# Deeper load buffers in the second expert layer, per-head softmax and early gathers in the routing of a diffusion block

## Chip, cores and metric

One core of a Trainium2 chip runs the whole program. The metric is the device time of one execution in microseconds: the median of three runs is 1841.48 us (1838.68 to 1842.52).

## What is computed

One layer of a diffusion backbone on 512 tokens of width 1024, all in float32. A mixing half (state space heads, long convolutions, output projection) comes first; nothing in it is touched. The second half is a product-key expert layer (PEER): each of 8 heads scores a token against two sets of 128 keys, takes the 16 best of each, the 16 best of the sums, and mixes 16 of 16384 one-neuron experts by a softmax:

```python
q = (hb @ wq).reshape(T, 8, 2, 128)
s1 = einsum('chd,hnd->chn', q[:, :, 0], k1);  s2 = einsum('chd,hnd->chn', q[:, :, 1], k2)
v1, i1 = top_k(s1, 16);  v2, i2 = top_k(s2, 16)
sc, ci = top_k(v1[..., :, None] + v2[..., None, :], 16)     # flattened
e = i1[ci // 16] * 128 + i2[ci % 16];  g = softmax(sc)
act = gelu(einsum('chkd,cd->chk', u_tab[e], hb))
out = einsum('chk,chkd->cd', g * act, v_tab[e])
```

## The kernel before, in words

The expert layer treats two groups of tokens in two ways.

**Tokens 0 to 127 are gathered.** There are 128 slots (8 heads by 16). `gathered(s)` lets GpSimd start an indirect DMA of one row of `uv` (u and v side by side, 8 KB) for each of 128 tokens, 1 MiB in all, into one of three buffers `uvr` (L1429). VectorE forms the dot product with `hrow` (L1430), ScalarE the GELU and the gate (L1433, L1435), VectorE adds the weighted v row to `accg` (L1438). All 128 slots must be done before the end; `gathers(share, after)` hands them out in fractions as the program goes.

**Tokens 128 to 511 are done densely**, over all 128 tiles of 128 experts. `first(i)` loads u tile i (512 KiB), splits it into a high part (ScalarE, L301) and a low part (VectorE, L302) and runs 24 matmuls into `pa` (L306 to L308), then a GELU. `second(i)` loads v tile i into `vr` (L1592), the gates `gc` of four tiles at a time (L1595) and, for a tile whose first layer ran earlier, the stored activations `gal` (L1602); it splits v into `vh` (ScalarE, L1598) and `vl` (VectorE, L1599), forms gate times activation (L1604), splits that into `wwh` and `wwl` (L1607, L1608) and runs 18 matmuls into six accumulators `pacc`.

Four stages follow each other:

1. Routing, eight heads (loop over `hd`): two projections `wq` of 24 matmuls, scores `psc` (L1482), `top16` and `pairs` on VectorE. After each head `run_ahead(RH)` issues `first` for tiles whose activations are stored in DRAM (`GA`), 6.3 a head. After the last head `run_ahead(RS)` adds 4 and one softmax covers all heads; only then is `gidx` (L1453) known and a gather possible.
2. Gates, 96 steps of four tokens: one-hot rows on VectorE and ScalarE (L1549 to L1556), eight matmuls `pgg` (L1558), an eviction to `gst` (L1560), `gathers(G_SHARE)` with 0.23 a step and `run_ahead(RG)` with 0.34 tiles a step. A `first` may come on TensorE no sooner than the `pgg` of three steps before.
3. The second layer over tiles 0 to 87, whose first layer ran ahead (`NRUN` = 88).
4. The second layer over tiles 88 to 127, each with its own `first`, begun two tiles earlier.

In stages 3 and 4 gathers are handed out at `left` a tile, times `R_RUN` in stage 3. `vr` and `gal` have two buffers each. All loads of `second` are issued by SyncE in program order, so a load that waits for its buffer holds back the loads behind it. The framework orders each engine's instructions by a planner with a timeline of its own, mostly in program order; a ready instruction may pass one that waits.

```python
left = (P - due[1] - N_SLACK) / (R_RUN * NRUN + (P - NRUN))
for i in range(P):
    while made < min(P, i + (AHEAD if i >= P - 1 - AHEAD else 2)):
        ready[made] = last_ga = first(made, V)
        made += 1
    last = second(i, ready.pop(i, None))
    gathers(left * (R_RUN if i < NRUN else 1.0) if i < P - 1 else P, last)
```

Of the kernel before, what the change touches and what calls it, by code (L numbers as in the profile page):

```python
# [9 lines left out]
F32 = mybir.dt.float32  # L10
F32R = mybir.dt.float32r
# [3 lines left out]
AF = mybir.ActivationFunctionType  # L15
ALU = mybir.AluOpType
AX = mybir.AxisListType

P = 128
D = 1024  # L20
# [51 lines left out]
          ("bglu", 4), ("gs5", 4), ("ghy", 4), ("negt", 4), ("a_re", 32), ("a_im", 32), ("lstep", 32))  # L72
NG = 128
SG = 32
NRUN = 88
NUV = 3
G_SHARE = 0.23
R_RUN = 0.4
ACT_OH = (2,1)
RG = 0.34  # L80
RH = 6.3
RS = 4
EQ_POOL = 3
G_LAG = 3
# [1 line left out]
ND = L - NG  # L86
# [5 lines left out]
QUIET = 1  # L92
WGT_ACT = 1
RGATE = 0
PERHEAD = 0
GH = 2.0
NOO = 3
S5M = 1
HYAT = 4
GCN = 4  # L100
FQ = 1
MERGE = 1
RECTS = ((0, 1, 16), (1, 1, 8), (2, 2, 5), (4, 4, 3), (8, 8, 1))
NCAND = 54 if MERGE else 50
NVR = 2
NVH = 3
VLV = 2
AHEAD = 2
# [119 lines left out]
def build(tc, I, out, dbg=None, stop=None):  # L228
# [64 lines left out]
    def sm(name, shape, dtype=F32, bufs=1, tag=None):  # L293
        return cur[0].tile(shape, dtype, tag=tag or name, name=name, bufs=bufs)

    def wblock(src, name, lo_eng=None):
# [4 lines left out]
        nc.scalar.activation(hi, raw, AF.Copy)  # L301
        (lo_eng or (nc.vector if FQ else nc.gpsimd)).tensor_tensor(lo, raw, hi.bitcast(F32), ALU.subtract)  # L302
        return hi.rearrange("p (k m) -> p k m", m=P), lo.rearrange("p (k m) -> p k m", m=P)
# [29 lines left out]
    V = nc.vector  # L333
    A = nc.scalar
    GP = nc.gpsimd
    FG = V if FQ else GP
    PE = nc.tensor
# [341 lines left out]
    for part in SEQ.split():  # L679
# [36 lines left out]
        elif part[0] == "S":  # L716
            t0, t1 = ((0, 4), None, (4, 6))[n_]
# [21 lines left out]
        elif part[0] == "P":  # L739
# [5 lines left out]
            if NWARM:  # L745
# [5 lines left out]
                for i in range(NWARM):  # L751
                    mm = PE.matmul(pwarm, warm[:, 0:P], warm, start=True, stop=True)
# [507 lines left out]
    for co in range(4):  # L1260
        wg = sg_(f"wg{co}", [P, 4, P], tag="wg", bufs=2)
        nc.sync.dma_start(wg, I["w_glu"][co].rearrange("p (k m) -> p k m", m=P))
        pg = ps5(f"pg{co}")
# [8 lines left out]
        t = g2_(f"cat5{co}", [P, 512])  # L1272
# [24 lines left out]
    for k in range(8):  # L1297
        t = b2(f"h2t{k}", [P, 512])
# [39 lines left out]
    iotak = sm("iotak", [P, P])  # L1338
# [17 lines left out]

    GA = dram.tile([NRUN, P, ND], F32, name="GA")

# [15 lines left out]
    def run_ahead(share):  # L1374
        ran[0] += share
        while ran[1] < min(NRUN, ran[0]):
            i = ran[1]
# [86 lines left out]
    for hd in range(8):  # L1464
# [20 lines left out]
        last = pairs(hd, val, idx)  # L1485
        if PERHEAD:
            softmax(hd)
            gathers(GH if hd else 0, last)
        run_ahead(RH)

# [4 lines left out]
    def columns(lt, eid, gt):  # L1495

        ei = sm(f"ei{lt}", [P, 2, P], I32, tag="ei", bufs=2)
        V.tensor_copy(ei[:, 0], eid)
        V.tensor_scalar(ei[:, 1], ei[:, 0], 127, None, ALU.bitwise_and)
        V.tensor_scalar(ei[:, 0], ei[:, 0], 7, None, ALU.logical_shift_right)  # L1500
        ef = sm(f"ef{lt}", [P, 2, P], tag="ef", bufs=2)
        V.tensor_copy(ef, ei)
        ptr = ps.tile([P, 512], F32, tag="psc", name=f"ptr{lt}", bufs=2 if RGATE else 3)[:, 0:3 * P].rearrange("p (e n) -> p e n", e=3)
        PE.transpose(ptr[:, 0], ef[:, 0], ident)
        PE.transpose(ptr[:, 1], ef[:, 1], ident)
        PE.transpose(ptr[:, 2], gt, ident)
        if RGATE:
            t = sm(f"cols{lt}", [P, 2, P], tag="cols", bufs=3)
            A.activation(t, ptr[:, 0:2], AF.Copy)
            g = sm(f"colg{lt}", [P, 2, P], F32R, tag="colg", bufs=3)  # L1510
            A.activation(g[:, 0], ptr[:, 2], AF.Copy)
            V.tensor_tensor(g[:, 1], ptr[:, 2], g[:, 0].bitcast(F32), ALU.subtract)
            return t, g.bitcast(F32)
        t = sm(f"cols{lt}", [P, 5, P], tag="cols", bufs=3)
        A.activation(t[:, 0:3], ptr, AF.Copy)
        A.activation(t[:, 3:5], ptr[:, 0:3:2], AF.Copy, scale=-1.0)
        return t

    def gates_r(b_, cols, c0):
        cols, g = cols  # L1520
        st = sm(f"gst{b_}", [P, P, SG], tag="gst", bufs=2)
        for q in range(SG // 4):
            pg = ps.tile([P, 4, 2, P], F32, tag="pgg", name=f"pgg{b_}_{q}", bufs=2)
            t0 = c0 + 4 * q
            oo = sm(f"oo{b_}_{q}", [P, 4, 2, P], F32R, tag="oo", bufs=NOO)
            os_ = sm(f"os{b_}_{q}", [P, 4, 2, P], F32R, tag="os", bufs=NOO)
            V.tensor_tensor(oo, iotak.unsqueeze(1).unsqueeze(1).broadcast_to((P, 4, 2, P)),
                            cols[:, :, t0:t0 + 4].rearrange("p e t -> p t e").unsqueeze(3).broadcast_to((P, 4, 2, P)), ALU.is_equal)
            for e in range(4):
                for h in range(2):  # L1530
                    A.activation(os_[:, e, h], oo[:, e, 0].bitcast(F32), AF.Copy, scale=g[:, h, t0 + e:t0 + e + 1])
            for e in range(4):
                mm = PE.matmul(pg[:, e].rearrange("p h i -> p (h i)"), oo[:, e, 1], os_[:, e].rearrange("p h i -> p (h i)"), start=True, stop=True)
            groups.append(mm)
            so = st[:, :, 4 * q:4 * q + 4]
            A.activation(so, pg[:, :, 0].rearrange("p t i -> p i t"), AF.Copy)
            last = V.tensor_tensor(so, pg[:, :, 1].rearrange("p t i -> p i t"), so, ALU.add)
            gathers(G_SHARE, last)
            run_ahead(RG)
        nc.scalar.dma_start(GD[b_], st)  # L1540

    def gates(b_, cols, c0):
        st = sm(f"gst{b_}", [P, P, SG], tag="gst", bufs=2)
        for q in range(SG // 4):
# [16 lines left out]
            gathers(G_SHARE, last)  # L1561
            run_ahead(RG)
        nc.scalar.dma_start(GD[b_], st)

    run_ahead(RS)
    if not PERHEAD:
        softmax(None)
# [5 lines left out]
    cols = [columns(lt, eids[:, lt], gts[:, lt]) for lt in range(1, 4)]  # L1573
    for lt in range(1, 4):
        for b_ in range(P // SG):
            (gates_r if RGATE else gates)((lt - 1) * (P // SG) + b_, cols[lt - 1], b_ * SG)
    run_ahead(NRUN)
    fr.close()
# [3 lines left out]
    mp = ms.enter_context(tc.tile_pool(name="mp", bufs=2))  # L1582
# [6 lines left out]
    def second(i, ga):  # L1589
        nonlocal gc  # L1590
        vr = mp.tile([P, D], F32, tag="vr", name=f"vr{i}", bufs=NVR)
        nc.sync.dma_start(vr, I["uv"][i * P:(i + 1) * P, D:2 * D])  # L1592
        if i % GCN == 0:
            gc = mp.tile([P, ND // SG, GCN, SG], F32, tag="gc", name=f"gc{i}")
            nc.sync.dma_start(gc, GD[:, :, i:i + GCN, :].rearrange("b p i t -> p b i t"))  # L1595
        vh = mp.tile([P, D], F32R, tag="vh", name=f"vh{i}", bufs=NVH)
        vl = mp.tile([P, D], F32R, tag="vl", name=f"vl{i}", bufs=NVH)
        A.activation(vh, vr, AF.Copy)  # L1598
        (V if QUIET or i >= P - VLV else GP).tensor_tensor(vl, vr, vh.bitcast(F32), ALU.subtract)  # L1599
        if ga is None:  # L1600
            ga = mp.tile([P, ND], F32, tag="gal", name=f"gal{i}")
            nc.sync.dma_start(ga, GA[i])  # L1602
        gw = mp.tile([P, ND], F32, tag="gw", name=f"gw{i}")
        V.tensor_tensor(gw.rearrange("p (b t) -> p b t", t=SG), ga.rearrange("p (b t) -> p b t", t=SG), gc[:, :, i % GCN], ALU.mult)  # L1604
        wh = mp.tile([P, ND], F32R, tag="wwh", name=f"wwh{i}", bufs=NVH)
        wl = mp.tile([P, ND], F32R, tag="wwl", name=f"wwl{i}", bufs=NVH)
        A.activation(wh, gw, AF.Copy)  # L1607
        last = V.tensor_tensor(wl, gw, wh.bitcast(F32), ALU.subtract)  # L1608
        held.append((i, wh, wl, vh, vl))
        if i < P - HOLD or i == P - 1:  # L1610
            for t in range(NT):
                ts_ = slice(t * P, (t + 1) * P)
                for e in range(2):
                    es_ = slice(e * 512, (e + 1) * 512)
                    for (n, ah_, al_, bh_, bl_) in held:
                        mm3(pacc[t][e], (ah_[:, ts_], al_[:, ts_]), (bh_[:, es_], bl_[:, es_]), n == 0, n == P - 1)
            held.clear()
        return last
# [4 lines left out]
    for e in range(2):  # L1623
# [5 lines left out]
        A.activation(gx2[:, e * 512:(e + 1) * 512], pgx, AF.Copy)  # L1629
    left = (P - due[1] - N_SLACK) / (R_RUN * NRUN + (P - NRUN))  # L1630
    ready = {}
    made = NRUN
    for i in range(P):
# [3 lines left out]
        last = second(i, ready.pop(i, None))  # L1637
        gathers(left * (R_RUN if i < NRUN else 1.0) if i < P - 1 else P, last)

# [4 lines left out]
    def residual(t):  # L1644
        xr = mp.tile([P, D], F32, tag="xf", name=f"xf{t}", bufs=4)
        nc.sync.dma_start(xr, X1R[t * P:(t + 1) * P])
        y = mp.tile([P, D], F32, tag="yf", name=f"yf{t}")
        ssq = mp.tile([P, 4], F32, tag="ssq", name=f"ssq{t}", bufs=4)
        for e in range(2):
            V.tensor_tensor(y[:, hs[e]], accg[:, hs[e]] if t == 0 else pacc[t - 1][e], gx2[:, hs[e]], ALU.mult)  # L1650
            (GP if t in T_ADD else V).tensor_tensor(xr[:, hs[e]], y[:, hs[e]], xr[:, hs[e]], ALU.add)
            A.activation(junk[:, hs[e]], xr[:, hs[e]], AF.Square, accum_out=ssq[:, e:e + 1])
        ends.append((xr, ssq))
# [44 lines left out]
```

## Time and profile before

| | |
|---|---|
| median of three runs | 1841.48 us |
| profiled execution | 1842.49 us |
| its span, first to last instruction | 1840.7 us |
| TensorE, matmul / weight load busy | 92% / 77% of the span |
| VectorE, ScalarE, GpSimd busy | 81%, 45%, 9% |
| DMA | 436.13 MB, mean 237 GB/s |
| mean granted TensorE clock | 0.968 of full speed |

The sum of the prediction is made against the profiled execution, which is 1.8 us longer than its span and 1.0 us longer than the median. "Busy" is the time in which at least one instruction of an engine ran; overlapping matmuls count once, so their pitch (start to start) is read from a timeline. A wait names the instruction that was late and what released it.

### The profile page before, as it was taken

How to read it: one execution, taken by the hardware profiler on the slowest of the kernel's cores; microseconds unless marked ns; L12 is line 12 of the kernel's file. 1: busy time of each engine (PE TensorE's matmuls, PEld its weight loads, DVE VectorE, ACT ScalarE, POOL GpSimd, SP SyncE). 2: the span in 40 equal slices, each digit the busy share in tenths (PEclk: the TensorE clock that was granted, in tenths of full speed). 3: DMA queues.
4: the chain of work that ended last, by engine and by line, in shares of the span. 5: the costliest groups of instructions: out<-in, count | busy, mean ns of one | idle time of the engine just before them, and what ended most of it. 6: DMA issues, size and time to landing. Idle time of an engine off the chain costs nothing.

```text
span 1840.7 us, 24953 instructions
## 1 busy us (share of the span) xinstructions
PE 1692.0 (92%) x8729; PEld 1420.7 (77%) x8731; DVE 1492.1 (81%) x3039; ACT 821.4 (45%) x1616; POOL 157.6 (9%) x158
## 2 busy tenths in 40 slices
PE   5799998879999999999999898989898898999997
PEld 2477654447799999989999886767676777999996
DVE  8866999967689988899999766777787777888886
ACT  3444453134533332348988633343333343444444
POOL 0000000000000000001101101111111112121211
PEclk9899998989899999999999998999999999999998
DMA  9436452322444444466898998999989888999981
GB/s 373 146 99 205 160 173 53 75 71 84 126 151 148 146 148 135 145 233 251 325 335 320 341 350 296 311 331 315 331 311 336 302 279 328 360 329 341 342 312 58
DMA packets 170228, 436.13 MB, mean 237 GB/s; under 512 B 17139, under 2 KB 102004, under 8 KB 150902
## 3 DMA queue, kind: packets, MB, share of 16 engines
q1 hardware_dynamic: 128854, 251.28, 40.6%
q0 software_dynamic: 18432, 134.23, 20.2%
q10 hardware_dynamic: 22816, 49.03, 7.3%
q8 instruction: 69, 1.13, 0.2%
q14 instruction: 57, 0.47, 0.1%
HBM read 381.52 MB, written 52.92 MB: 236 GB/s over the span
## 4 chain that ended last, share of the span: by engine, by line
PE 47%; DVE 13%; DMA 13%; ACT 2%; issue 2%; DVEq 0%; ACTq 0%; SPq 0%
DMA vr<-in_uv_dram 11%; PE pa L308 7%; PE pa L306 6%; PE pa L307 6%; PE pacc L307 5%; PE pacc L306 5%; PE pgg L1558 5%; PE pacc L308 5%; DVE vl L1599 2%; PE pq L308 2%; PE pq L306 2%; PE pq L307 2%; ACT vh L1598 2%; DVE idx L1351 1%; DVE rs L1349 1%
## 5 line engine op out<-in xcount | busy, mean ns | idle before, releaser
L307 PE MATMUL pacc<-vl,wwh 128*128 128x512 f32 x768 | 305.8, 399 | 4.7 <-DVE vl L1599 4.7
L308 PE MATMUL pacc<-vh,wwl 128*128 128x512 f32 x768 | 298.0, 397 | 0.0
L306 PE MATMUL pacc<-vh,wwh 128*128 128x512 f32 x768 | 237.1, 402 | 42.8 <-ACT vh L1598 42.7
L1429 POOL DMA_INDIRECT uvr<-in_uv_dram,gidx x128 | 145.2, 1134 | 1148.1 <-DVE accg L1438 810.5
L1599 DVE TENSOR_TENSOR vl<-vr,vh 128x1024 fp32r<-128x1024 f32 x128 | 156.1, 1222 | 94.8 <-ACT vh L1598 94.6
L306 PEld LDWEIGHTS pacc<-vh,wwh 128*128 128x128 f32 x768 | 144.7, 192 | 83.2 <-ACT vh L1598 55.2
L1598 ACT ACTIVATE vh<-vr 128x1024 fp32r<-128x1024 f32 x128 | 135.0, 1057 | 162.3 <-DMA vr<-in_uv_dram 126.5
L307 PEld LDWEIGHTS pacc<-vl,wwh 128*128 128x128 f32 x768 | 148.0, 193 | 38.1 <-DVE vl L1599 7.4
L308 PEld LDWEIGHTS pacc<-vh,wwl 128*128 128x128 f32 x768 | 147.6, 192 | 31.1
L1438 DVE SCALAR_TENSOR_TENSOR accg<-uvr,wgt,accg 128x1024 f32<-128x1024 f32 x128 | 163.7, 1279 | 4.0 <-ACT wgt L1435 1.2
L1430 DVE SCALAR_TENSOR_TENSOR junk<-uvr,hrow 128x1024 f32<-128x1024 f32 x128 | 155.9, 1218 | 2.2 <-DMA uvr<-in_uv_dram,gidx 2.2
L1607 ACT ACTIVATE wwh<-gw 128x384 fp32r<-128x384 f32 x128 | 66.5, 520 | 131.7 <-PE pacc L307 92.3
L1558 PE MATMUL pgg<-o,o 128*128 128x128 f32 x768 | 95.3, 278 | 4.3 <-ACT o L1554 4.3
L1558 PEld LDWEIGHTS pgg<-o,o 128*128 128x128 f32 x768 | 94.3, 195 | 4.5 <-ACT o L1554 4.5
L1608 DVE TENSOR_TENSOR wwl<-gw,wwh 128x384 fp32r<-128x384 f32 x128 | 70.8, 553 | 32.8 <-ACT wwh L1607 32.7
L1549 DVE TENSOR_TENSOR o<-iotak,cols 128x512 f32<-128x512 f32 x96 | 65.9, 686 | 10.3 <-PE pgg L1558 10.3
L1556 DVE TENSOR_SCALAR o<-iotak,cols 128x128 f32<-128x128 f32 x240 | 70.2, 343 | 0.0
L1433 ACT ACTIVATE wgt<-dots 128x1 f32<-128x1 f32 x128 | 25.4, 199 | 87.4 <-DVE junk L1430 87.1
L1554 ACT ACTIVATE o<-o,cols 128x128 f32<-128x128 f32 x144 | 63.6, 493 | 0.2
L1368 ACT ACTIVATE ga<-pa 128x384 f32<-128x384 f32 x128 | 60.4, 472 | 2.7 <-PE pa L308 2.7
L1560 ACT ACTIVATE gst<-pgg 128x512 f32<-128x512 f32 x96 | 56.7, 591 | 2.5 <-PE pgg L1558 2.2
L1604 DVE TENSOR_TENSOR gw<-gal,gc 128x384 f32<-128x384 f32 x88 | 48.4, 553 | 9.1 <-DMA gal<-GA 8.6
(1812 smaller groups left out, 4141.4 us busy)
## 6 DMA issues: line engine op xcount, KB each, us to landing
vr<-in_uv_dram SPq DMA_DIRECT2D x128, 512.0 KB
GD<-gst ACTq DMA_DIRECT2D x12, 2048.0 KB
gc<-GD SPq DMA_DIRECT2D x32, 768.0 KB
GA<-ga ACTq DMA_DIRECT2D x88, 192.0 KB
gal<-GA SPq DMA_DIRECT2D x88, 192.0 KB
wb<-in_w_ada_dram SPq DMA_DIRECT2D x32, 512.0 KB
wa<-in_w_ada_dram SPq DMA_DIRECT2D x8, 1024.0 KB
KD<-kk SPq DMA_DIRECT2D x16, 256.0 KB
```

The costliest lines, as they stand in the source:

```text
L306: nc.tensor.matmul(o, a[0], b[0], start=start, stop=False)
L307: nc.tensor.matmul(o, a[0], b[1], start=False, stop=False)
L308: nc.tensor.matmul(o, a[1], b[0], start=False, stop=stop_)
L1429: GP.indirect_dma_start(out=uvr, out_offset=None, in_=I["uv"], in_offset=bass.IndirectOffsetOnAxis(ap=gidx[:, s:s + 1], axis=0))
L1430: ins = V.scalar_tensor_tensor(junk, uvr[:, 0:D], 1.0, hrow, ALU.mult, ALU.mult, accum_out=dots[:, s:s + 1])
L1438: V.scalar_tensor_tensor(accg, uvr[:, D:2 * D], wgt[:, s:s + 1], accg, ALU.mult, ALU.add)
L1556: last = V.tensor_scalar(o1[:, e], iotak, cols[:, 0, t:t + 1], cols[:, 2, t:t + 1], ALU.is_equal, ALU.mult)
L1558: mm = PE.matmul(pg[:, e, :], o2[:, e], o1[:, e], start=True, stop=True)
L1598: A.activation(vh, vr, AF.Copy)
L1599: (V if QUIET or i >= P - VLV else GP).tensor_tensor(vl, vr, vh.bitcast(F32), ALU.subtract)
L1607: A.activation(wh, gw, AF.Copy)
L1608: last = V.tensor_tensor(wl, gw, wh.bitcast(F32), ALU.subtract)
```

## The change

The constants are edited, `PERHEAD` is switched on, `gal` gets four buffers by `NGAL` and `vr` four by `NVR`; the residual's `yf` (two buffers of its own before) now takes turns in those of `vr`. `gates_r` and the branch of `columns` under `RGATE` are rewritten too, but `RGATE` stays 0, so neither is called.

```diff
-NRUN = 88
+NRUN = 92
-R_RUN = 0.4
+R_RUN = 0.35
-RG = 0.34
-RH = 6.3
+RG = 0.4
+RH = 7
-PERHEAD = 0
-GH = 2.0
+PERHEAD = 1
+GH = 3
+NGAL = 4
-NVR = 2
+NVR = 4
...
         if RGATE:
...
     def gates_r(b_, cols, c0):
...
         if ga is None:
-            ga = mp.tile([P, ND], F32, tag="gal", name=f"gal{i}")
+            ga = mp.tile([P, ND], F32, tag="gal", name=f"gal{i}", bufs=NGAL)
             nc.sync.dma_start(ga, GA[i])
...
-        y = mp.tile([P, D], F32, tag="yf", name=f"yf{t}")
+        y = mp.tile([P, D], F32, tag="vr", name=f"yf{t}", bufs=NVR)
```

With `PERHEAD` the loop over heads runs, after `pairs(hd)`, the softmax of that head alone (six VectorE operations and an Exp) and `gathers(3 if hd else 0, last)`; the softmax over all heads at the end falls away. `GH` was without effect before.

## Rows read from the trace of the kernel before

**Rows 1.** The page's slices: GB/s moved in each of 40 equal slices.

```profile
GB/s 373 146 99 205 160 173 53 75 71 84 126 151 148 146 148 135 145 233 251 325 335 320 341 350 296 311 331 315 331 311 336 302 279 328 360 329 341 342 312 58
```

**Rows 2.** Busy time by stage: routing, gates, turn, run tiles, tiles with their own first.

```profile
core 0: us, PE busy (x) PEld busy (x) DVE busy (x) ACT busy (x) POOL busy (x), PEclk, DMA share, GB/s
488.00:806.00 318.00, 314.81 (x1738) 297.49 (x1736) 279.21 (x991) 103.68 (x141) 0.38 (x2) 1.00 0.44 145
806.00:1047.00 241.00, 236.48 (x1618) 235.84 (x1617) 227.19 (x466) 204.44 (x507) 30.22 (x26) 0.99 0.85 313
1047.00:1062.00 15.00, 6.15 (x32) 5.61 (x31) 2.28 (x6) 2.03 (x3) 0.29 (x1) 0.81 0.92 322
1062.00:1500.00 438.00, 396.63 (x1682) 320.47 (x1682) 318.62 (x428) 162.20 (x287) 52.27 (x51) 0.96 0.93 321
1500.00:1820.00 320.00, 313.80 (x1556) 282.28 (x1555) 256.83 (x321) 141.00 (x268) 62.43 (x51) 0.99 0.85 305
```

**Rows 3.** Waits between 1062 and 1535 us: total us, times, longest.

```profile
ACT vh L1598 <- DMA vr<-in_uv_dram: 124.3, 61, 9.6
PE pacc L306 <- ACT vh L1598: 42.7, 27, 5.5
```

**Rows 4.** Waits of SyncE's DMA queue between 1062 and 1535 us.

```profile
SPq L1592 <- DVE vl L1599: 151.4, 79, 5.8
```

**Rows 5.** Chain of waits near 1340 us: start, us, what.

```profile
1339.63 1.24 DVE vl L1599
1340.88 6.26 DMA vr<-in_uv_dram
1347.16 1.07 ACT vh L1598
```

**Rows 6.** Busy time by stage, instructions on the tile pacc alone.

```profile
1062.00:1500.00 438.00, 372.22 (x1539) 294.35 (x1540) 0.00 (x0) 0.96 0.93 321
1500.00:1820.00 320.00, 175.60 (x729) 137.54 (x728) 0.00 (x0) 0.99 0.85 305
```

**Rows 7.** Timeline of TensorE: the first matmuls of tiles 94 and 95, and one of pacc before.

```profile
1541.00 0.40 PE L306 MATMUL pacc<-vh,wwh 128*128 128x512 f32 x1
...
1542.37 0.33 PE L306 MATMUL pa<-h2h,u94h 128*128 128x384 f32 x1
...
1546.55 0.33 PE L306 MATMUL pa<-h2h,u95h 128*128 128x384 f32 x1
```

**Rows 8.** Busy time in two heads of six run-ahead tiles each, columns as rows 2.

```profile
563.00:639.60 76.60, 76.01 (x418) 71.50 (x417) 70.44 (x250) 23.44 (x32) 0.00 (x0) 1.00 0.44 145
```

**Rows 9.** Waits of VectorE in the routing, 488 to 806 us.

```profile
DVE val L1346 <- PE psc L1482: 23.4, 8, 3.0
```

**Rows 10.** Groups of the page: the two VectorE passes of a gather.

```profile
L1438 DVE SCALAR_TENSOR_TENSOR accg<-uvr,wgt,accg 128x1024 f32<-128x1024 f32 x128 | 163.7, 1279 | 4.0 <-ACT wgt L1435 1.2
L1430 DVE SCALAR_TENSOR_TENSOR junk<-uvr,hrow 128x1024 f32<-128x1024 f32 x128 | 155.9, 1218 | 2.2 <-DMA uvr<-in_uv_dram,gidx 2.2
```

**Rows 11.** Timeline of the softmax over all heads, and a VectorE cast of 64 elements.

```profile
798.84 1.28 ACT L1447 ACT_TABLE_LOAD   x1
798.87 0.67 DVE L1446 TENSOR_TENSOR GX<-SC 128x512 f32<-128x512 f32 x1
...
799.46 0.19 DVE L1412 CAST posf<-pos 128x64 f32<-128x64 uint32 x1
...
800.13 0.63 ACT L1447 ACTIVATE GX<-GX 128x512 f32<-128x512 f32 x1
```

**Rows 12.** Gates: two pieces of the chain of waits (start, us).

```profile
921.60 2.68 PE pgg L1558 x24
928.47 2.68 PE pgg L1558 x24
```

**Rows 13.** Gates: VectorE's one-hot rows, a group of the page and a timeline piece.

```profile
L1549 DVE TENSOR_TENSOR o<-iotak,cols 128x512 f32<-128x512 f32 x96 | 65.9, 686 | 10.3 <-PE pgg L1558 10.3
...
901.56 0.85 DVE L1556 TENSOR_SCALAR o<-iotak,cols 128x128 f32<-128x128 f32 x3
```

More of the change, by code (lines that the diff above doesn't have):

```diff
@@ L1507, in columns @@
         if RGATE:
[L1508 to L1513, printed above, removed]
+            t = sm(f"cols{lt}", [P, P], tag="cols", bufs=3)
+            A.activation(t, ptr[:, 1], AF.Copy)
+            gh_ = sm(f"colg{lt}", [P, P], F32R, tag="colg", bufs=3)
+            A.activation(gh_, ptr[:, 2], AF.Copy)
+            V.tensor_tensor(ptr[:, 2], ptr[:, 2], gh_.bitcast(F32), ALU.subtract)
+            return t, gh_.bitcast(F32), ptr
         t = sm(f"cols{lt}", [P, 5, P], tag="cols", bufs=3)
@@ L1519, in gates_r, with per_token @@
     def gates_r(b_, cols, c0):
-        cols, g = cols
+        i2, gh_, ptr = cols
         st = sm(f"gst{b_}", [P, P, SG], tag="gst", bufs=2)
+        def per_token(x, t0):
+            return x[:, t0:t0 + 4].unsqueeze(2).broadcast_to((P, 4, P))
         for q in range(SG // 4):
@@ L1524, in gates_r @@
             t0 = c0 + 4 * q
-            oo = sm(f"oo{b_}_{q}", [P, 4, 2, P], F32R, tag="oo", bufs=NOO)
+            o2 = sm(f"o2_{b_}_{q}", [P, 4, P], F32R, tag="o2", bufs=NOO)
+            o1 = sm(f"o1_{b_}_{q}", [P, 4, P], tag="o1", bufs=NOO)
             os_ = sm(f"os{b_}_{q}", [P, 4, 2, P], F32R, tag="os", bufs=NOO)
-            V.tensor_tensor(oo, iotak.unsqueeze(1).unsqueeze(1).broadcast_to((P, 4, 2, P)),
-                            cols[:, :, t0:t0 + 4].rearrange("p e t -> p t e").unsqueeze(3).broadcast_to((P, 4, 2, P)), ALU.is_equal)
+            keys_ = iotak.unsqueeze(1).broadcast_to((P, 4, P))
+            GP.tensor_tensor(o2, keys_, per_token(i2, t0), ALU.is_equal)
+            V.tensor_tensor(o1, keys_, per_token(ptr[:, 0], t0), ALU.is_equal)
+            V.tensor_tensor(os_[:, :, 1], o1, per_token(ptr[:, 2], t0), ALU.mult)
             for e in range(4):
-                for h in range(2):
-                    A.activation(os_[:, e, h], oo[:, e, 0].bitcast(F32), AF.Copy, scale=g[:, h, t0 + e:t0 + e + 1])
+                A.activation(os_[:, e, 0], o1[:, e], AF.Copy, scale=gh_[:, t0 + e:t0 + e + 1])
             for e in range(4):
-                mm = PE.matmul(pg[:, e].rearrange("p h i -> p (h i)"), oo[:, e, 1], os_[:, e].rearrange("p h i -> p (h i)"), start=True, stop=True)
+                mm = PE.matmul(pg[:, e].rearrange("p h i -> p (h i)"), o2[:, e], os_[:, e].rearrange("p h i -> p (h i)"), start=True, stop=True)
             groups.append(mm)
```

## The prediction, made before the changed kernel was run

> **What bounds the kernel now.** I read the slices first for where the DMA engines are loaded: in the second half they move 280 to 360 GB/s, in the routing 135 to 150 [rows 1]. Then the busy times by stage [rows 2]. In routing and gates TensorE is busy 99% and 98% of the time: it sets the pace, with VectorE close behind, 88% in the routing and 94% in the gates. From 1062 to 1500 us, over the tiles that ran ahead, no engine is full: DMA 0.93, TensorE 91% by matmul busy but 73% by weight loads. From 1500 us on, where each tile brings its own `first`, TensorE is at 98%.
>
> The third view was the list of waits of that middle stage. ScalarE's `vh` waited 124.3 us for `vr` to land, and TensorE 42.7 us for `vh` [rows 3]; SyncE in turn stood 151.4 us before issuing `vr`, for the `vl` that frees a buffer [rows 4]. The chain shows the loop: `vl` 1.24, load 6.26, `vh` 1.07 us, in all 8.6 us for a buffer, and two buffers give 4.3 us a tile at best [rows 5]. ScalarE waited up to 9.6 us for one load [rows 3], so the average is worse: 1539 matmuls of `pacc` by 1500 us are 85.5 tiles [rows 6], and after an 11 us start they took 427 us: 4.99 us a tile. The last term is TensorE's own price. From 1541.00 to 1542.37 us six matmuls of `pacc` start before the first of tile 94 [rows 7]: a pitch of 0.228 us, and 18 make 4.11 us. A `first` takes 1546.55 - 1542.37 = 4.18 us [rows 7]; of all the matmuls in this stage 143 are not of `pacc` [rows 2, 6], some 5 of them `first` tiles that the planner moved up, two in the start and about 3.5 after it.
>
> **Edit 1, gathers and softmax in the routing.** Heads 1 to 7 each issue three gathers: 21. One costs VectorE 1.22 + 1.28 = 2.50 us [rows 10], three 7.5. A head's softmax is six VectorE operations on 64 elements or fewer; the nearest row has 0.19 us for 64 [rows 11], so about 1.1 us. `RH` 7 makes 56 tiles instead of 51 (0.3 x 8 rounded up): 5 x 4.18 = 21 us of TensorE, and 1.1 us of VectorE for each further low part. A head with six tiles lasts 38.3 us, VectorE busy 35.2 of them [rows 8]. With seven tiles TensorE needs 42.5 us, and VectorE 35.2 + 1.1 + 7.5 + 1.1 = 44.9: **VectorE becomes the bound of the routing.** It can use the 3 us in which it now waits for each head's scores, 23.4 us in all [rows 9], since the gathers stand just there. So 42.5 for head 0 and 7 x 45 = 357.5 us against 318: **+40 us**. Bounds: +23 if VectorE's extra work all found room beside TensorE's; +66 if none of it did (21 x 2.50 + 5 x 1.1 + 8 x 1.1). I stand nearer the middle, since [rows 8] leave VectorE no more than 3 us a head.
>
> The rest of this edit has cover. The 21 MiB of gathers find DMA 0.44 loaded [rows 2]. GpSimd's queue is empty there, and its issue waits for a free `uvr`, so the load runs ahead of the dot product; without that cover a head would wait the length of a load. ScalarE gets an Exp and two table loads of 1.28 us [rows 11] in each head, 2.8 us where it idles two thirds of the time [rows 2]; behind them in its queue are the `uh` casts, which run a tile ahead (rival 4). The old softmax's 2.8 us of VectorE drop out; they are in the 1.1 us a head only roughly, and I leave that inside the bounds.
>
> **Edit 2, RG 0.4.** Before, 55 tiles were done ahead of the gates and 33 in them, the last in step 96. Now 60 are, and 32 more at 0.4 a step end in step 78. Two clumps of three steps stand 6.87 us apart, 2.68 of it `pgg` [rows 12]: 0.89 us of TensorE a step, and 4.19 for a `first`. Steps 1 to 78 take 78 x 0.89 + 32 x 4.19 = 203.5 us. The last 18 have nothing to fill TensorE; VectorE needs 0.69 + 2.5 x 0.28 [rows 13] + 0.23 x 2.50 = 1.97 us each, 35.5 in all. Together 239 against 96 x 0.89 + 33 x 4.19 = 224: **+15 us**. Bounds 0 (the `first` tiles slip back into the empty steps) and +22 (the steps' round trip shows as well).
>
> **Edit 3, the second layer over run tiles.** 44 gathers are done before it instead of 23, so `left` falls from 112/75.2 = 1.489 to 91/68.2 = 1.334, and a run tile carries 0.467 gathers instead of 0.596. Its DMA falls from 512 + 192 + 192 + 610 KiB (1.54 MB) to 512 + 192 + 192 + 478 (1.41 MB). Four buffers let four loads be under way: a loop of 8.6 to 11 us then serves four tiles and the wait for depth is gone. What is late next is either TensorE, 4.11 us, or the DMA engines: at the 321 GB/s of this stage [rows 2] 1.41 MB is 4.4 us, at the 350 of the best slice inside it [rows 1] 4.0. VectorE, 319 of 438 us busy there [rows 2], loses work and has room. With four more tiles run ahead the stage holds 89.5 tiles and the same 3.5 `first`: on TensorE alone 89.5 x 4.11 + 3.5 x 4.18 = 382 us. I take 395, 3% over that because two resources are both nearly full: 4.41 us a tile. 395 - 427 = **-32 us**, bounds -45 (TensorE alone) and -18 (89.5 x 4.57, the rate of rival 2). The matmul busy of [rows 2] would leave only 41 of 438 us to win. By the Trainium skill (Perfetto Trace Analysis, Identifying the Most-Contended Engine) pipelined matmuls make that busy time a bad measure of headroom and the weight loads' a better one. The pitch of [rows 7] agrees; with the busy time a tile could not go below (427 - 41) / 85.5 = 4.51 us, 404 us in all, and the sum would be 9 us higher.
>
> **Edit 4, NRUN 92.** Four tiles fewer come with their own `first` in the last stage, which TensorE sets: 4 x (4.18 + 4.11) = **-33 us**. Its DMA per tile falls too (1.334 gathers), so it stays with TensorE.
>
> **Costing nothing.** `RGATE` is 0, so the new `gates_r` is not run. `yf` in `vr` buffers comes when all tiles are consumed; four instead of two may save 1 us at the end. The turn at 1047 to 1062 us is a wait for the last gate write and stays.
>
> **Sum.** +40 + 15 - 32 - 33 = -10 us on the profiled 1842.5 us: 1832.5, and 1 us less against the median: 1831.5.
>
> **Rivals.**
> 1. *Better overlap:* VectorE's work fits into its idle time and TensorE sets every stage: +30, +5, -45, -33, in all -43: 1798.5 us. For it: each of VectorE's waits in the routing is a hole where a gather fits [rows 9]. Against: VectorE at 94% and TensorE at 98% in the gates already [rows 2].
> 2. *Bandwidth, not depth:* the loads take 6 us because the DMA engines are shared, and four at a time only wait in the engines instead of in SyncE's queue. The stage keeps its rate, 1.54 MB in 4.99 us or 309 GB/s: 1.41 MB is 4.57 us, the run stage gives -18, total +4: 1845.5 us, no difference. For it: DMA 0.93 busy [rows 2]. Against: slices at 350 [rows 1], and SyncE idle 151 us [rows 4].
> 3. *Slower, VectorE in the routing:* the gathers stand in line with `top16`, whose results the next matmuls need, and nothing is absorbed: +66 instead of +40, total +16: 1857.5 us. It decides as soon as the routing grows by more than 50 us, what the two later terms win (65) less the gates' 15. For it: VectorE is over its budget by [rows 8]; against: the hole of 3 us a head.
> 4. *Slower, table loads:* two in each head hold up the `uh` casts and so TensorE: 7 further heads x 2.8 = 20 us, total +10: 1851.5 us. Against: ScalarE's idle two thirds. In the trace a load of 1.28 us is followed by the Exp at once [rows 11]. The Trainium skill (ScalarE: Activation LUTs, What ACT_TABLE_LOAD costs) adds a drain of 1.38 us to each switch; by it this rival would cost some 37 us, but no drain is seen here.
> 5. *Not what it says:* the planner may push the gathers out of the routing into the gates, where VectorE is full: +23 + 15 + 52 - 65 = +25: 1866.5 us.
>
> **Chances.** Forecast 0.48 (1816 to 1844), rival 1 0.18, rival 2 0.14, rival 3 0.14, rivals 4 and 5 0.03 each. This kernel's measurement can tell 0.2%, 3.7 us, from no change. Faster by more: 0.8 of the forecast and all of rival 1, with a little of rival 2, 0.58; within it: 0.13; slower: half of rival 2, rivals 3 to 5 and a little of the forecast, 0.29. The range runs from just below rival 1 to rival 3 and leaves out what goes beyond them: 1796 to 1859 us.
>
> **What would show it.** Right: the routing 350 to 365 us with VectorE over 95% and TensorE near 93%; in the gates VectorE's share falls only after the last `first`, TensorE's drops to half; in the run stage the wait of `vh` for `vr` falls below 30 us, DMA at 0.95 or more and a tile at 4.3 to 4.5 us. Wrong: TensorE still at 98% in the routing (rival 1), 4.57 us a tile with DMA at 0.93 (rival 2), `top16` waiting behind gathers and the routing over 372 us (rival 3), casts waiting behind table loads (rival 4).

## The result, and the profile after

The changed kernel takes 1786.41 us, the median of four runs (1783.61 to 1788.32), against 1841.59 us before: a ratio of 0.970, 95% interval 0.9685 to 0.9719. It is 55 us faster; 10 us were forecast, and the time lies below the range. The profiled execution has a span of 1786.5 us. Of all executions in this study one, of the experiment e4, took 9376.75 us, five times its others; it is left out of that row.

To see where the time went, both profiles are cut at the same events. First the kernel after, instructions by tile: the first `pq` matmul begins the routing, the first `pgg` the gates, the last `gst` ends them, the first and the last `pacc` bound the second layer (durations are min/median/max in ns, then first and last start).

```profile
L307 PE MATMUL pq<-h2h,wq0h x8: 387/398/792, 483.9 to 495.1; 128*128 128x512 f32 x8
...
L1566 PE MATMUL pgg<-o,o x768: 270/275/551, 861.6 to 1085.8; 128*128 128x128 f32 x192
L1568 ACT ACTIVATE gst<-pgg x96: 575/592/628, 863.7 to 1086.3; 128x512 f32<-128x512 f32 x96
...
L307 PE MATMUL pacc<-vh,wwh x768: 387/389/402, 1111.9 to 1774.0; 128*128 128x512 f32 x192
```

The same view of the kernel before:

```profile
L306 PE MATMUL pq<-h2h,wq0h x8: 389/398/796, 479.5 to 491.0; 128*128 128x512 f32 x8
...
L1558 PE MATMUL pgg<-o,o x768: 270/275/580, 828.4 to 1046.7; 128*128 128x128 f32 x192
L1560 ACT ACTIVATE gst<-pgg x96: 577/590/599, 830.6 to 1047.0; 128x512 f32<-128x512 f32 x96
...
L306 PE MATMUL pacc<-vh,wwh x768: 386/389/795, 1073.7 to 1828.2; 128*128 128x512 f32 x192
```

| us | front | routing | gates | turn | second layer | tail | span |
|---|---|---|---|---|---|---|---|
| before | 479.5 | 348.9 | 218.6 | 26.7 | 754.5 | 12.5 | 1840.7 |
| after | 483.9 | 377.7 | 224.7 | 25.6 | 662.1 | 12.5 | 1786.5 |
| difference | +4.4 | +28.8 | +6.1 | -1.1 | -92.4 | 0 | -54.2 |

Nothing in the front was changed; over the 13 profiles of this study it lies between 478.5 and 483.9 us, so its 4.4 us are scatter. The cut differs from [rows 2], where the routing ends 22 us before the first `pgg`. The rest is a loss of 35 us in routing and gates and a win of 92 us in the second layer. The busy times by stage of the kernel after answer to [rows 2]; they are the 22 us before the gates, the gates, the turn, and the second layer cut near its last run-ahead tiles (columns as there).

```profile
839.20:861.60 22.40, 16.52 (x94) 15.67 (x93) 22.40 (x36) 12.06 (x26) 1.68 (x1) 0.93 0.50 167
861.60:1086.30 224.70, 218.59 (x1494) 216.27 (x1494) 208.91 (x440) 193.17 (x487) 26.07 (x23) 0.98 0.85 311
1086.30:1111.90 25.60, 17.09 (x85) 16.49 (x86) 10.83 (x18) 8.27 (x14) 2.88 (x2) 0.80 1.00 360
1111.90:1518.00 406.10, 406.10 (x1808) 337.92 (x1807) 326.47 (x435) 169.81 (x295) 58.06 (x47) 1.00 0.99 349
1518.00:1774.70 256.70, 256.70 (x1294) 232.86 (x1292) 194.85 (x244) 110.10 (x206) 39.08 (x36) 1.00 0.75 268
```

From its first to its last `pacc` TensorE is not idle once, and the list of waits has none of it there. The granted clock is 1.00, the full 2.4 GHz, over the run tiles, where it was 0.96 before [rows 2], and the DMA engines move 349 GB/s at a share of 0.99 where they moved 321 at 0.93. In the chain of waits, cut to these run tiles, the reload of `vr` was nearly half before and is gone. The summary of the kernel before between 1100 and 1500 us (first items):

```profile
by line: DMA vr<-in_uv_dram 48.2%; PE pacc L307 8.9%; PE pacc L306 8.6%; PE pacc L308 8.1%; DVE vl L1599 7.2%; ACT vh L1598 6.3%; issue 5.3%; DVE junk L1430 1.7%; DMA gal<-GA 1.3%; DVE gw L1604 1.2%; ACT wwh L1607 1.1%; DVE wwl L1608 0.9%; 
```

and of the kernel after, 1120 to 1500 us:

```profile
by line: PE pacc L309 32.4%; PE pacc L308 32.4%; PE pacc L307 32.4%; PE pa L307 1.0%; PE pa L309 0.9%; PE pa L308 0.9%
```

The waits of that stage answer to [rows 3]: `vh` waits 6.7 us for `vr` (1111 to 1518 us) in place of 124.3. What ScalarE waits for now is TensorE, to free a buffer of `wwh`.

```profile
ACT wwh L1615 <- PE pacc L308: 156.6, 88, 3.9
...
ACT vh L1606 <- DMA vr<-in_uv_dram: 6.7, 3, 3.3
```

### The profile page after: what moved, and what is told of

It is laid out like the page before. It is cut to its first block, busy times and chain, and to the rows that moved or that the text cites. A ratio compares the mean times of both kernels' runs of the same rounds, so it can differ in the third digit from the quotient of the medians.

```text
span 1786.5 us, 25056 instructions
## 1 busy us (share of the span) xinstructions
PE 1675.2 (94%) x8731; PEld 1416.4 (79%) x8731; DVE 1495.4 (84%) x3081; ACT 840.0 (47%) x1637; POOL 166.2 (9%) x158
## 4 chain that ended last, share of the span: by engine, by line
PE 77%; DVE 15%; DMA 5%; issue 2%; ACT 2%; SPq 0%; ACTq 0%; DVEq 0%
PE pacc L308 10%; PE pacc L309 10%; PE pacc L307 10%; PE pa L309 8%; PE pa L307 8%; PE pa L308 8%; PE pgg L1566 4%; PE pq L307 1%; PE px L307 1%; PE pq L308 1%; PE px L309 1%; PE pq L309 1%; PE px L308 1%; PE pmodr L641 1%; DMA wb<-in_w_ada_dram 1%
## 5 line engine op out<-in xcount | busy, mean ns | idle before, releaser
L308 PE MATMUL pacc<-vl,wwh 128*128 128x512 f32 x768 | 299.3, 390 | 0.0
L1430 POOL DMA_INDIRECT uvr<-in_uv_dram,gidx x128 | 153.8, 1202 | 1069.2 <-DVE accg L1439 881.2
L307 PE MATMUL pacc<-vh,wwh 128*128 128x512 f32 x768 | 246.5, 389 | 0.0
L308 PEld LDWEIGHTS pacc<-vl,wwh 128*128 128x128 f32 x768 | 144.1, 188 | 29.7
L307 PEld LDWEIGHTS pacc<-vh,wwh 128*128 128x128 f32 x768 | 144.1, 188 | 28.9
L1566 PE MATMUL pgg<-o,o 128*128 128x128 f32 x768 | 99.2, 282 | 9.7 <-DVE o L1557 7.0
L1557 DVE TENSOR_TENSOR o<-iotak,cols 128x512 f32<-128x512 f32 x96 | 65.6, 683 | 15.7 <-PE pgg L1566 15.7
```

The costliest lines, as they stand in the source:

```text
L307: nc.tensor.matmul(o, a[0], b[0], start=start, stop=False)
L308: nc.tensor.matmul(o, a[0], b[1], start=False, stop=False)
L1430: GP.indirect_dma_start(out=uvr, out_offset=None, in_=I["uv"], in_offset=bass.IndirectOffsetOnAxis(ap=gidx[:, s:s + 1], axis=0))
L1566: mm = PE.matmul(pg[:, e, :], o2[:, e], o1[:, e], start=True, stop=True)
```

## The experiments

Eleven runs, each on top of before or after; e11 is the kernel after once more. One table of their stages first, cut at the events above; ratios are to the kernel before measured beside each group, which took 1847.65 us beside e1 to e4, 1848.09 beside e5 to e8 and 1844.71 beside e9 to e11.

| us | routing | gates | turn | second layer | tail | span | median | ratio (95%) |
|---|---|---|---|---|---|---|---|---|
| e1 buffers alone | 349.0 | 218.6 | 26.9 | 698.9 | 12.6 | 1788.0 | 1789.01 | 0.968 (0.964 to 0.972) |
| e2 two buffers | 377.3 | 225.2 | 25.9 | 702.0 | 12.8 | 1823.9 | 1824.23 | 0.987 (0.983 to 0.992) |
| e3 two `gal` | 376.7 | 225.5 | 24.4 | 665.8 | 12.5 | 1785.7 | 1790.34 | 0.969 (0.965 to 0.973) |
| e4 no gathers in heads | 369.4 | 223.0 | 25.9 | 678.0 | 21.5 | 1800.2 | 1799.46 | 0.973 (0.968 to 0.978) |
| e5 88 tiles ahead | 368.9 | 218.3 | 27.7 | 679.4 | 12.5 | 1788.9 | 1788.08 | 0.968 (0.965 to 0.971) |
| e6 even gates | 376.3 | 215.6 | 31.3 | 661.2 | 12.5 | 1776.6 | 1778.93 | 0.965 (0.960 to 0.970) |
| e7 five gathers a head | 409.2 | 224.6 | 25.7 | 661.8 | 12.6 | 1812.4 | 1815.62 | 0.984 (0.980 to 0.987) |
| e8 three buffers | 377.3 | 224.9 | 25.8 | 664.7 | 12.5 | 1785.3 | 1788.92 | 0.970 (0.966 to 0.973) |
| e9 two gathers, 88 ahead | 354.0 | 218.2 | 25.8 | 683.0 | 12.6 | 1773.9 | 1776.58 | 0.963 (0.961 to 0.965) |
| e10 one gather, 88 ahead | 347.0 | 218.0 | 23.9 | 690.5 | 12.5 | 1774.8 | 1775.47 | 0.963 (0.960 to 0.965) |
| e11 change again | 376.3 | 225.5 | 24.4 | 662.1 | 12.5 | 1782.9 | 1784.38 | 0.967 (0.965 to 0.969) |

### Depth or bandwidth: e1 and e2

e1, on the kernel before:

```diff
-NVR = 2
+NVR = 4
-        ga = mp.tile([P, ND], F32, tag="gal", name=f"gal{i}")
+        ga = mp.tile([P, ND], F32, tag="gal", name=f"gal{i}", bufs=4)
-    y = mp.tile([P, D], F32, tag="yf", name=f"yf{t}")
+    y = mp.tile([P, D], F32, tag="vr", name=f"yf{t}", bufs=NVR)
```

> The kernel before with only the buffers of the change: four for vr, four for gal, yf in those of vr. Depth theory (two buffers made the second layer wait for the round trip of a reload): TensorE then runs without a gap wherever the DMA engines can follow. A run tile still carries 0.596 gathers, 1.54 MB, which at the 350 GB/s of the changed kernel's run stage is 4.4 us against 4.1 of TensorE, so of the 76 us that TensorE stood in the second layer some 25 stay: about 1790 us, with the wait of vh for vr still seen, DMA at 0.97 or more. Bandwidth theory (the fewer gathers a tile freed the DMA engines, depth only moves the wait into them): the stage stays near 5 us a tile, 1832 us or more.

e2, on the kernel after, the same lines the other way:

```diff
-NVR = 4
+NVR = 2
-NGAL = 4
+NGAL = 2
-    y = mp.tile([P, D], F32, tag="vr", name=f"yf{t}", bufs=NVR)
+    y = mp.tile([P, D], F32, tag="yf", name=f"yf{t}")
```

> The changed kernel with two buffers again for vr, gal and yf; everything else as changed. Depth theory: the reload loop comes back, 4.5 us or more a run tile against 4.08, 90 tiles by 0.5 us and some 12 us in the tiles after: about 1835 us, vh waiting for vr over 80 us. Bandwidth theory: 1.41 MB a tile is light enough for two buffers, at most 1795 us.

e1 came out at 1789.01 us where depth said 1790: the buffers alone take 55.6 us off the second layer and touch nothing else. The first 400 us of the second layer in e1, busy times, and then two waits of its whole second layer:

```profile
1076.50:1476.50 400.00, 387.58 (x1716) 319.33 (x1715) 330.31 (x442) 163.90 (x300) 66.26 (x54) 1.00 1.00 359
```

```profile
PE pacc L306 <- ACT vh L1598: 9.4, 7, 1.4
ACT vh L1598 <- DMA vr<-in_uv_dram: 6.5, 3, 5.4
```

The same two views of e2:

```profile
1109.10:1509.10 400.00, 375.56 (x1608) 304.33 (x1607) 288.95 (x386) 150.37 (x258) 43.71 (x40) 0.98 0.92 313
```

```profile
ACT vh L1606 <- DMA vr<-in_uv_dram: 123.0, 66, 5.3
PE pacc L307 <- ACT vh L1606: 25.9, 16, 4.1
```

With two buffers the DMA engines stand at 0.92 and 313 GB/s though each tile carries less; with four they reach a share of 1.00 and 359 GB/s, though each carries more. So the 0.93 of [rows 2] was not a limit of the engines: the loop of the reload did not ask for more. The Trainium skill (DMA: Bandwidth & Descriptors, Specifications) puts the limit of HBM for a core at about 358 GB/s; the 359 of e1 and 358 of the first 400 us in e4 agree with it as means over 400 us. It is no ceiling for a shorter stretch: a slice of 45 us of the kernel after reads 386 GB/s.

The traffic is not nothing, though. e2 came out at 1824.23 us, between the 1835 of depth and the 1795 of bandwidth. It keeps the lighter tiles and loses 40 us in the second layer against after, not the 56 that depth had put on it; against before it still wins 52.5 us there. Part of that is fewer `first` tiles. The weight loads of `pa` in the second layer, 24 a tile, are 912 before and 795 after, and 795 in e2 too:

```profile
1073.70:1828.20 754.50, 167.47 (x913) 160.42 (x912) 18.39 (x39) 0.98 0.88 311
```

```profile
1111.90:1774.00 662.10, 145.67 (x797) 139.80 (x795) 16.13 (x34) 1.00 0.90 318
```

The difference is 4.9 tiles or 20 us, which by subtraction leaves 32 us to the lighter tiles, even with two buffers. Of a stall of some 72 us (92.4 less 20) the buffers alone remove 56 and the lighter tiles alone 32, and both together all of it.

e1 has as many `first` tiles as before and keeps 698.9 - 662.1 - 20 = 16 us of gaps. The depth theory had put 25 there and laid them to full engines moving 1.54 MB a tile. That is not shown. TensorE's longest waits in e1 are eight of 1.3 to 1.4 us. From 1076 to 1500 us its chain of waits holds two loads (`gc` 7.7 and `gal` 2.0 us) and none of `vr`, and most of the eight look like this:

```profile
1259.50 0.24 PE pacc L307
1259.77 0.52 ACT wwh L1607
1260.29 0.96 ACT vh L1598
1261.29 1.65 PE pacc L306 x6
```

ScalarE ran the next `vh` behind a `wwh` that itself waited for TensorE to free a buffer, while `vh` waited for a load in three places only, 6.5 us in all. The order of ScalarE's instructions is thus a rival of bandwidth for these 16 us, and no run tells the two apart.

### How deep, and which: e3 and e8

```diff
# e3
-NGAL = 4
+NGAL = 2
# e8
-NVR = 4
+NVR = 3
-NGAL = 4
+NGAL = 3
```

> The changed kernel with two buffers for gal alone; vr keeps four. If depth counts, SyncE's order counts too: the load of gal two tiles ahead waits for gw and stands before the next vr in the queue, so the third and fourth vr buffer are never filled early: 1800 to 1835 us. If only the depth of vr counts, 1786 to 1792 us.

> The changed kernel with three buffers for vr and gal. Depth theory: a reload loop of 8.6 to 11 us serves three tiles, 2.9 to 3.7 us a tile, under TensorE's 4.08: at most 1792 us. If the longest loads count (9.6 us of waiting, seen before), some gaps stay: 1795 to 1810 us.

Both leave the second layer within 4 us of after (665.8 and 664.7). The idea that SyncE's queue order would make the third and fourth `vr` buffer useless with two `gal` fell: VectorE does wait for `gal`, 23.7 us in all, but the waits of TensorE in the second layer sum to 2.1 us. Three buffers are enough for the time, with `vh` waiting 28.4 us for `vr`. The rows of e3 and then of e8:

```profile
DVE gw L1612 <- DMA gal<-GA: 23.7, 23, 2.3
```

```profile
ACT vh L1606 <- DMA vr<-in_uv_dram: 28.4, 19, 4.4
```

### What the gathers cost the routing: e4, e7, e9, e10

```diff
# e4
-GH = 3
+GH = 0
# e7
-GH = 3
+GH = 5
# e9, e10
-NRUN = 92
+NRUN = 88
-RG = 0.4
+RG = 0.34
-RH = 7
+RH = 6.3
-GH = 3
+GH = 2        # e10: 1
```

> The changed kernel with no gather in the routing (0 a head instead of 3); the softmax stays in each head, so left rises to 112/68.2 = 1.642 and a run tile carries 0.575 gathers. If TensorE sets the routing also with the gathers in it, the routing shrinks by under 10 us, while the second layer pays for 1.52 MB a run tile at 350 GB/s, 4.34 us against 4.08, and 2.97 MB in each later tile, 360 GB/s: about 1805 us. If the gathers cost the routing more than they bring (52 us of VectorE work in a full engine), 1780 us or less.

> The changed kernel with five gathers a head instead of three, 35 in the routing instead of 21. TensorE already sets the second layer, so nothing is won there. If VectorE is the bound of the routing at three gathers, 14 more cost 14 x 2.5 = 35 us: about 1820 us. If it still has room, at most 1795 us.

> The changed kernel with two gathers a head, 88 tiles ahead as before (6.3 a head, 0.34 a gate step), R_RUN 0.35 and all the buffers. If VectorE sets the routing at three gathers and TensorE with fewer, the routing falls from 369 us (three gathers, same tiles) to 349 to 353, the gates stay at 218, and the second layer at 679 to 685, since a run tile carries 1.43 MB: 1768 to 1778 us, faster than the changed kernel by 10 us or more. If something else in the heads holds the routing (the softmax, the table loads, the gathers' issue), it stays over 362 us: 1783 us or more.

> The same with one gather a head. If TensorE sets the routing from two gathers down, it gains nothing more there (348 to 351 us), and the second layer pays for seven more gathers, 1.46 MB a run tile: 680 to 690 us, in all 1770 to 1780 us, level with two gathers or a little slower. If VectorE still sets at two, seven gathers fewer are worth up to 17 us in the routing: 1755 to 1765 us.

The routing stage of before, of after and of e4, busy times with the columns of [rows 2], one fence each:

```profile
479.50:828.40 348.90, 341.24 (x1872) 321.43 (x1871) 307.83 (x1044) 120.97 (x173) 4.60 (x5) 0.99 0.46 152
```

```profile
483.90:861.60 377.70, 366.40 (x2009) 345.55 (x2010) 359.35 (x1142) 158.32 (x244) 30.64 (x24) 0.99 0.59 203
```

```profile
482.40:851.80 369.40, 365.29 (x2012) 345.83 (x2012) 317.81 (x1098) 149.81 (x209) 6.50 (x5) 0.99 0.45 152
```

Without gathers the routing is 369.4 us, 20.5 above before. The further `first` tiles alone would make it 24. The weight loads of `pa` ahead of the first `pgg`, 24 a tile, show 56 tiles before (1344), 62 after (1488) and 61.8 in e4 (1483): six more, where the prediction counts five. So the softmax by head and its table loads cost no time on balance, with the softmax over all heads gone from the end. The rows of before, after and e4:

```profile
479.50:828.40 348.90, 240.35 (x1344) 232.02 (x1344) 26.42 (x56) 0.99 0.46 152
```

```profile
483.90:861.60 377.70, 266.90 (x1488) 256.71 (x1488) 29.43 (x62) 0.99 0.59 203
```

```profile
482.40:851.80 369.40, 265.84 (x1483) 255.82 (x1483) 28.51 (x61) 0.99 0.45 152
```

The 21 gathers then add 8.3 us, in line with the forecast that has TensorE set the routing with them too (under 10), though they put 359.35 - 317.81 = 41.5 us of work on VectorE. Fourteen more (e7) add 31.5, 2.25 us each, close to the 2.50 that a gather keeps VectorE busy: from three a head on, VectorE is the bound. Where the overrun shows is at the end. TensorE stays fed through the heads and then stands, before the gates, until VectorE has caught up. In e7 the last 47 us of the routing have VectorE busy 44.91 and TensorE 20.67, and the longest wait of TensorE in the stage is one of 23.3 us:

```profile
840.00:887.00 47.00, 20.67 (x118) 19.94 (x116) 44.91 (x104) 16.29 (x37) 12.86 (x6) 0.75 0.59 215
```

```profile
PE ptr L1505 <- DVE ef L1503: 23.3, 1, 23.3
```

With 88 tiles ahead the routing reads 368.9 (three gathers, e5), 354.0 (two) and 347.0 us (one): 2.1 us a gather from three to two, 1.0 from two to one; the routing of the six profiles with the same routing code as after reads 376.3 to 377.7, so the steps are clear of the scatter. At one a head it is as short as with none before. So VectorE still set a little at two a head, and e10 won 7 us where no gain was expected if TensorE set from two down, but the second layer gave the 7 us back (690.5 against 683.0). Of these some 4 are one `first` more behind the first `pacc` (936 weight loads of `pa` against 912), so the seven gathers that moved there cost 3 at most.

e4 also shows why the gathers are taken early: with all 128 left to gates and second layer, that layer takes 16 us more and the tail 9. The tail is longer because gathers are still landing when TensorE is done; the 16 us are gaps of the kind that e1 has, with the same two readings. Two pieces of the chain of waits at the end of e4:

```profile
1768.60 5.82 DMA uvr<-in_uv_dram,gidx
...
1776.35 1.30 DVE accg L1439
```

### The tiles run ahead: e5 and e6

```diff
# e5
-NRUN = 92
+NRUN = 88
-R_RUN = 0.35
+R_RUN = 0.4
-RG = 0.4
+RG = 0.34
-RH = 7
+RH = 6.3
# e6
-RG = 0.4
+RG = 0.335
```

> The changed kernel with the run-ahead settings of before (88 tiles, 6.3 a head, 0.34 a step, R_RUN 0.4); gathers in the heads, per-head softmax and buffers stay. If TensorE sets the routing, it shrinks by five first tiles, 21 us, the gates are filled to the end (6 us won), and the second layer grows by four first tiles, 17 us: 1776 to 1786 us. If VectorE sets the routing, it shrinks by only the five low parts, 6 us, and the second layer still grows by 17: about 1791 to 1797 us.

> The changed kernel with 0.335 run-ahead tiles a gate step instead of 0.4, so that the 32 tiles last through all 96 steps. If the empty last 18 steps are what the gates lost, TensorE is full to the end: 96 x 0.89 + 32 x 4.18 = 219 us against 225 measured, 1780 us. If VectorE sets the gates anyway, no difference, 1786 us.

e5 lies between the two forecasts, level with the change: routing 8.8 us shorter (the VectorE forecast was 6, that of TensorE 21), gates 6.4 shorter, second layer 17.3 longer, front 1.8 shorter, turn 2.1 longer. Four tiles more or fewer ahead win nothing once TensorE sets the second layer, for a `first` then costs the same at either place. e6 spreads the same 32 tiles over all 96 gate steps: 215.6 us against 224.7, so the empty last steps cost 9 us. Its turn is 5.7 us longer, for a reason left open, so 3 us are won. The median of 1778.93 agrees with the 1780 expected, but a front 4.2 us shorter than in the profile of after has a part in it.

### The change on the same chip: e11

> The changed kernel once more, beside the two above on one chip: 0.970 of the kernel before, about 1787 us where that takes 1842, with the stages of the first profile: routing 378, gates 225, second layer 662 us.

As expected, 0.967. Beside its 1784.38 us, e9 and e10 took 1776.58 and 1775.47: both beat the changed kernel by 8 to 9 us (10 or more were expected of e9) and before by 3.7%. They keep all the buffers, 88 tiles ahead and one or two gathers a head. e1's interval overlaps both intervals of the change: the buffers alone cannot be told from the whole change.

## Why the prediction was wrong

The direction was right and the mechanism named. The size was off in three terms, all the same way: 27, 11 and 9 us, of which front and turn give 3 back.

**Edit 3, with edit 4: -65 forecast, -92.4 measured.** The failing step is "I take 395, 3% over that because two resources are both nearly full". Nothing was lost to the two being full: TensorE was busy 406.1 of 406.1 us, and not by that measure alone. 1715 `pacc` matmuls in 400 us of the kernel after (less 63 of `pa`, 11 us) give a pitch of 0.227 us. Rival 1 had this part: its -45 - 33 = -78 is TensorE alone. The other 14 us are found in three places, which sum to 16 by rounded terms. The pitch of 0.227 instead of 0.228 gives 2 us, and 4.9 `first` tiles fewer instead of 4 give 4.

The third place is the stage after 1500 us, called TensorE's on its busy share of 98% [rows 2], the very measure that the prediction had set aside one stage earlier. By pitch its 42.5 tiles and 34.5 `first` tiles need 765 x 0.227 + 34.5 x 4.18 = 318 us of the 328 to its last `pacc`: 10 us of stall that the buffers removed too. They stand almost all in one place, the start of that stage (kernel before, all instructions):

```profile
1529.00:1535.00 6.00, 0.47 (x4) 0.14 (x2) 0.23 (x3) 1.15 (x2) 0.00 (x0) 0.92 0.77 315
1535.00:1541.00 6.00, 5.53 (x13) 4.03 (x13) 6.00 (x7) 3.80 (x7) 1.68 (x1) 0.51 0.45 124
1541.00:1600.00 59.00, 59.00 (x299) 53.66 (x298) 51.23 (x64) 26.00 (x51) 14.85 (x11) 1.00 0.96 359
```

TensorE stood 5.5 us for a `vh` and then ran six more at a granted clock of 0.51, the level of 1.2 GHz, its `pacc` matmuls 0.43 us apart. From 1541 us to the last `pacc` its matmuls start without a gap, so the rest of the stage was TensorE's as predicted. A wait thus cost more than its own length: part of the gain is the granted clock, 0.96 over the run tiles before and 1.00 after.

The order of the limits was read rightly. The loop of [rows 5] was the limit and the DMA engines were not; worked out from it, the buffers alone should have taken 51 us off the second layer (76 less 25), and in e1 they took 55.6. That the two are so near is in part luck: the stall was 72 us rather than 76, and the 16 us that stayed are not shown to be bandwidth.

**Edit 1: +40 forecast, +28.8 measured.** The price of a head was right: 45 us forecast, and the cast that ends each head's search (L1413) shows 7 heads in 314.3 us, 44.9 each. The row after, then the row before:

```profile
L1413 DVE CAST posf<-pos x8: 182/189/199, 522.3 to 836.6; 128x64 f32<-128x64 uint32 x8
```

```profile
L1412 DVE CAST posf<-pos x8: 186/196/198, 518.2 to 799.5; 128x64 f32<-128x64 uint32 x8
```

That VectorE set this price is less sure: TensorE was 99% busy there, since three further `first` tiles moved from the end into these heads (1256 weight loads of `pa` against 1178 in e4).

The failing step is "42.5 for head 0 and 7 x 45 = 357.5 us against 318". Before, those seven heads took 281.3 us and not the 278 that the base leaves them, so they grow by 33.0, not 37, though six tiles more ran ahead of the gates and not five. Head 0 did not grow: from the first `pq` to this cast it took 38.7 us before and 38.4 after, since the tiles issued behind it run in the next head. From the last cast to the gates it fell from 28.9 to 25.0 us. That end holds a `first` less, and the softmax over all heads no longer stands there (the 2.8 us that the text left "inside the bounds"); the two are not separated. VectorE as the new bound was right, but only by 8 us over TensorE (e4), and the holes of [rows 9] did take gathers: the waits for `psc` fell from 23.4 to 6.1 us. By the prediction's own signs the routing went to rival 1: in the cut of [rows 2] it took 346.9 us, under the 350 to 365 named, with TensorE still at 98%.

**Edit 2: +15 forecast, +6.1 measured.** Steps 1 to 78 went as worked out: the last `first` ended near 1059.4 us, 198 us into the gates (203.5 forecast, with 32 tiles where 30 fell there). The failing step is "VectorE needs ... 1.97 us each, 35.5 in all" for the last 18. They took 26.9 us. The stretch, all instructions and then `pgg` alone:

```profile
1059.40:1086.30 26.90, 20.79 (x146) 18.51 (x144) 26.31 (x62) 25.16 (x69) 3.23 (x3) 0.94 0.80 294
```

```profile
1059.40:1086.30 26.90, 20.76 (x144) 18.51 (x144) 0.94 0.80 294
```

TensorE did 144 `pgg` matmuls, 18 steps, but VectorE had one-hot rows for 14 left (`L1557`, one a step): it was four steps ahead by its buffers when the tiles ran out. The price was right, 14 x 1.97 = 27.6 us; the count of steps was not.

```profile
1059.40:1086.30 26.90, 9.55 (x14) 0.94 0.80 294
```

**Rivals.** Rival 1, TensorE setting every stage, is what happened in the second layer. Its +30 and +5 for routing and gates came within 1.2 us, but by luck: the prediction's own bound for that case was +23, e4 has 20.5 without gathers, and VectorE put 8 us on top. Its 1798.5 is 12 us too long, mainly for the reasons under edit 3. Rival 2 (bandwidth) falls by e1. Rival 3 (nothing absorbed) falls by e4: 41.5 us of VectorE's work cost 8.3. Rival 4 (table loads) falls by e4 too. The pair in one head of the kernel after:

```profile
657.13 1.28 ACT L1448 ACT_TABLE_LOAD   x1
658.42 0.26 ACT L1448 ACTIVATE GX<-GX 128x64 f32<-128x64 f32 x1
658.70 1.28 ACT L1369 ACT_TABLE_LOAD   x1
659.99 0.49 ACT L1369 ACTIVATE ga<-pa 128x384 f32<-128x384 f32 x1
```

Each instruction follows the one before within 0.03 us, and the two loads and the Exp take 2.8 us in an engine with room. The drain that the Trainium skill adds to a switch (ScalarE: Activation LUTs, What ACT_TABLE_LOAD costs) does not appear. Rival 5 did not happen: 18 of the 21 gathers were done inside the heads and three before the gates.

## What to carry over

A load wait beside DMA engines at 0.93 is a question of depth until shown otherwise: work out the loop (free, reload, first use) divided by the buffers, and if it is near the time of a tile, one more buffer comes first; here three did. Read TensorE's room from the pitch of its matmuls in every stage, also in one that looks full at 98%, and look where in the stage the gap stands. Moving work into an earlier stage pays only up to the room left there: the first gather a head was free, the second cost 1.0 us, the third 2.1, and the run-ahead of four more tiles won nothing once the buffers had made the later stage run at TensorE's pace.

## Not expected of the hardware

The second layer ran 662 us with TensorE full while the DMA engines stood at 0.99 in its first part, so there two resources near their limit cost each other nothing. In the seven heads TensorE and VectorE ran side by side at 99% and 97% (309.82 and 304.29 of 314.3 us), and the price, 8 us, came mostly behind them. The untouched front differs by up to 5.4 us between profiles of kernels that are the same there.
